# A hybrid decoder layer in one kernel: the beginning rebuilt, later GpSimd low parts, and GpSimd in the last scaling

## The chip, the cores and the metric

The kernel runs on one core of one Trainium2 chip. The metric is the time of one execution on the device in microseconds, median of several runs. Engines are named as in the profile: PE is TensorE's matmul (PEld its weight load), DVE VectorE, ACT ScalarE, POOL GpSimd, SP the engine that issues most transfers. Transfers are issued from SP's and from ACT's queue.

## What is computed

One layer of a hybrid decoder on x of 1024 tokens by 1024 channels, in float32:

```
h    = rmsnorm(x) * norm1_w
proj = h @ w_in                                  # q, k, v, z of mixer A; b, a; q, k, v of mixer B
A    = gated delta rule over 4 heads of 128: causal conv of width 4 and silu on q, k, v,
       l2norm of q and k, decay and beta per head, a triangular solve in each chunk,
       then rmsnorm times silu(z)
B    = attention over 8 heads of 64 in three dilated windows, merged by their denominators
x    = x + concat(A, B) @ w_out
u    = causal conv of width 3 over (rmsnorm(x) * norm2_w) @ w_up
x    = x + (silu(u_gate) * u_up) @ w_down
out  = rmsnorm(x) * final_norm_w
```

## The kernel before

All work lies with channels on the 128 partitions and tokens along the row; x comes transposed, as eight tiles of 128 x 1024. A float32 product is made from three products in a faster format: each operand is split into a high part (ACT copies it into that format) and a low part (the rest, a subtraction on DVE or POOL), and `mm3` (L200) adds high x high, high x low and low x high into a bank of PSUM. "Low part" below means the second.

**The order of the work.** Each engine runs its instructions in the order in which they were laid down. For PE that order is planned by the class `Weave` (L49): each part of the layer is a generator, which yields the time until its next product can run, and `Weave` picks by level and time. It keeps a model of the time: a product adds its `us` to PE's (`product`, L91); an operation on another engine adds an estimate to that engine's (`account`, L81; the estimates are in `Engine`, L124, and L151 to L158). So a changed estimate, or an operation given to another engine, can move products in PE's order anywhere behind it. On the other engines a scheduler orders by need; `after(inst, anchor)` (L189) forces one instruction behind another of the same engine, `ua` and `uv` (L154) are ACT and DVE with a raised priority.

**The beginning** (L242 to L365). SP issues norm1_w (`n1`), the first half of the first weights (`w0`, three column tiles of keys), the first x tile in two halves, the second half of the weights, and then x tiles and weights by turns. For each x tile, `split_x` (L286) makes `xhi` on ACT (scaled by n1) and `xlo` on DVE; ACT squares the tile and DVE adds it to `acc`, the sum of squares. Meanwhile PE multiplies a tile of ones 18 times (L351, the tile `warm`), which serves no result. `first` (L357) is the product of the first three key columns: for each of the eight x tiles six banks, three products each. `norms` (L371) turns `acc` into the reciprocal root of the mean square: a product with ones, a power on POOL, and a transposed broadcast that DVE copies into `rstdB` (L389). The columns leave their banks multiplied by `rstdB` (`scaled`, L445, the tiles `xr`), and only then are the banks free for the next columns.

**The dense columns** (`dense`, L498). 29 weights follow, in the order of `DENSE` (L45): one key, eight quarter weights for the values of mixer B, then q and v of the four heads by turns, the columns of attention, and z. `take` (L516) prepares the next weight while the present one is multiplied; from place 9 its low part is made by POOL (`spare`, L222), before that by DVE. Between the columns PE does what the planner puts there: transposes and small products of the delta rule (`kprep`, `qprep`, `vprep`, L602 and on), later attention. `forward_sub` inverts the triangles of all heads and chunks at once in 62 dependent DVE operations on two tiles in SBUF, `tmp` and `xi`, which interleave with the convolutions and the emptying of banks.

**The end** (`mlp_down`, L1535). The last product runs in halves of 256 tokens of the first 512. For each of eight channel tiles DVE adds the bank to x, ACT squares it, and the squares are added up (`complete`, L1486). `mean_of` (L1497) and `turned` (L1510) leave the reciprocal root, spread over the partitions, in a bank. `scale_out` (L1516) multiplies each of the eight pieces (128 x 256) by the final norm's weight `fw` and by that bank, one DVE operation each, and issues its transfer; for the last eight pieces the transfers go by turns to SP's and to ACT's queue.

Of the kernel before, what the change touches and what calls it, by code (L numbers as in the profile page):

```python
# [147 lines left out]
def hybrid_layer(tc, I, out):  # L148
# [93 lines left out]
    n1 = const("n1", [P, KT], I["n1"])  # L242
# [43 lines left out]
    def split_x(xt, k, sl):  # L286
        hi, lo = xs[k]
        ac.activation(hi[:, sl], xt[:, sl], AF.Copy, scale=n1[:, k:k + 1])
        ve.scalar_tensor_tensor(lo[:, sl], xt[:, sl], n1[:, k:k + 1], hi[:, sl].bitcast(F32), op0=OP.mult,
                                op1=OP.subtract)  # L290

    for k in range(KT):
        xt = A("xt", ("kT*", "dv*")[k % 2])
        xts.append(xt)
        if k % 2 == 0:
            wst = tile_(wp, [P, 2, 384], F32, "wst", "wst", 2)
            whi, wlo = [A(nm, "uy", F32R, (P, 2, 384)) if k < 4 else A(nm, "kt", F32R, (P, 2, 384))
                        for nm in ("whi", "wlo")]
            wk0.append((whi, wlo))
        xs.append((X("xhi"), X("xlo")))  # L300
        if k == 0:
            sy.dma_start(wst[:, 0, :], I["w0"][0, :, 0])
            for h in range(2):
                sy.dma_start(xt[:, half(h)], I["xT"][:P, half(h)])
            sy.dma_start(wst[:, 1, :], I["w0"][0, :, 1])
            split(wst[:, 0, :], whi[:, 0, :], wlo[:, 0, :])
            for h in range(2):
                split_x(xt, 0, half(h))
            split(wst[:, 1, :], whi[:, 1, :], wlo[:, 1, :])
        else:  # L310
            if k % 2 == 0:
                sy.dma_start(wst, I["w0"][k // 2])
            sy.dma_start(xt, I["xT"][k * P:(k + 1) * P, :])
            if k % 2 == 0:
                wlast = split(wst, whi, wlo)
            split_x(xt, k, slice(0, S))
        sq = A("sq", "qa")
        ac.activation(sq, xt, AF.Square)
        if k == 0:
            sq0 = sq  # L320
        elif k == 1:
            ve.tensor_tensor(acc, sq0, sq, op=OP.add)
        else:
            inst = ve.tensor_tensor(acc, acc, sq, op=OP.add)
            if k == 6:
                after(inst, first_lo, "the products wait for these weights")
        if k == 4:
            first_lo = wlast
# [22 lines left out]
    for _ in range(18):  # L351
        mm(wbank[:, :P], warm, warm, 0.3)
# [4 lines left out]
    def first():  # L357
        for k in range(KT):
            w = wk0[k // 2]
            for i in range(6) if k else (0, 2, 4, 1, 3, 5):  # L360
                yield wv.need(*xs[k], *w)
                m, h = divmod(i, 2)
                wm = [t[:, k % 2, m * P:(m + 1) * P] for t in w]
                mm3(pst[i], wm, [t[:, half(h)] for t in xs[k]], k == 0, k == KT - 1)
# [6 lines left out]
    def norms():  # L371
        yield wv.need(acc, slack=8.0)
# [125 lines left out]
    def dense():  # L498
# [17 lines left out]
        def take():  # L516
            w = nxt.pop()
            i = place[0] = place[0] + 1
            if i < len(srcs):
                nxt.append(weight(None, st=raw.pop(), spare=i >= 9))  # L520
# [965 lines left out]
    def complete(m, hh, sl, apart=False):  # L1486
# [4 lines left out]
        ac.activation(sq[:, sl] if m else rstdB[:, sp_], x, AF.Square)  # L1491
# [24 lines left out]
    def scale_out(hh, sl, pb, ms=range(8), queues=(sy,), anchor=None):  # L1516
        for m in ms:
            x = x1h[m][:, part(m, hh, sl)]
            inst = ve.scalar_tensor_tensor(x, x, fw[:, m:m + 1], pb[:, :sl.stop - sl.start], op0=OP.mult, op1=OP.mult)
# [15 lines left out]
    def mlp_down():  # L1535
# [36 lines left out]
        left, right = slice(0, 256), slice(256, 512)  # L1572
        for i in range(4):
# [10 lines left out]
        scale_out(0, right, turned(mean_of(0, right, "hf", more), right, "ch"), queues=(sy, sa))  # L1584
# [72 lines left out]
```

## Time and profile before

| | us |
|---|---|
| runs, median of 3 | 1204.37 (1203.77 to 1204.42) |
| the profiled execution's own time | 1206.67 |
| its span, from the first to the last instruction | 1204.6 |

The times in all lines are from that one profiled execution. A line of the timeline gives start, duration, engine, source line, operation, the tile written and those read, shapes, and in brackets how long the engine had been idle before and what ended it. Source lines are often those of a helper (L142 and L144 stand for every operation given to DVE, ACT, POOL and the queues; L193 for products, L197 for transposes), so tiles tell more than lines. In a table of windows a row gives the window, its length, then busy time and instructions of PE, PEld, DVE, ACT and POOL, the granted clock of PE (1.00 is full), the share of the DMA engines and GB/s.

### The profile page before, as it was taken

What the parts mean: (1) busy time and instruction counts of PE and PEld (TensorE: products, weight loads), DVE (VectorE), ACT (ScalarE), POOL (GpSimd) and SP (SyncE); (2) the same over time, 40 slices, a digit from 0 to 9 for tenths busy, and PEclk for the clock granted to TensorE, in tenths of its full rate; (3) what the DMA queues carried; (4) which work ended last, traced back from release to release, by engine and by line L of the source; (5) the groups of instructions that cost most, each with busy time, mean ns of one, the idle gap of its engine ahead of it and who ended that gap; (6) DMA issues with size and microseconds to landing.
All of it is one profiled execution on the core that took longest, in us unless ns stands there. A gap on an engine that the chain in (4) does not pass through costs nothing.

```text
span 1204.6 us, 18326 instructions
## 1 busy us (share of the span) xinstructions
PE 1191.6 (99%) x7068; PEld 987.0 (82%) x7068; DVE 916.1 (76%) x1442; ACT 575.3 (48%) x1126; POOL 108.2 (9%) x98
## 2 busy tenths in 40 slices
PE   9999999999999999999999999999999999999997
PEld 7888778889877778888888888888888888888886
DVE  7583985656365466767989989889898889999875
ACT  7375335456355443655545544444454454444441
POOL 0313232213422110000000000000000000000000
PEclk9999999999999999999999999999999999999998
DMA  7434233435624304444213122131322298547513
GB/s 235 107 93 121 103 109 119 149 115 164 222 94 128 95 36 120 169 140 140 84 56 106 58 100 91 67 105 53 105 73 85 94 370 305 180 162 226 165 54 140
DMA packets 85798, 154.80 MB, mean 129 GB/s; under 512 B 21168, under 2 KB 36304, under 8 KB 85712
## 3 DMA queue, kind: packets, MB, share of 16 engines
q1 hardware_dynamic: 85136, 153.12, 39.1%
q8 instruction: 55, 0.90, 0.3%
q10 hardware_dynamic: 576, 0.52, 0.1%
q14 instruction: 31, 0.25, 0.1%
HBM read 117.68 MB, written 35.93 MB: 128 GB/s over the span
## 4 chain that ended last, share of the span: by engine, by line
PE 93%; DVE 4%; ACT 1%; issue 1%; DMA 1%; SPq 0%; POOLq 0%; POOL 0%; DVEq 0%; ACTq 0%
PE ps L193 43%; PE pa L193 20%; PE dw L193 17%; PE pc L193 10%; PE ps L197 3%; DVE tmp L142 1%; DVE xi L142 1%; PE warm L193 1%; ACT sm L144 0%; DMA mt<-mdram 0%; DVE xr L142 0%; DVE qT L142 0%; DVE vT L142 0%; DMA mdram<-um 0%; DVE x1h L142 0%
## 5 line engine op out<-in xcount | busy, mean ns | idle before, releaser
L193 PE MATMUL dw<-pr 128*128 128x512 f32 (+1 forms) x984 | 211.3, 376 | 0.0
L193 PEld LDWEIGHTS dw<-pr 128*128 128x128 f32 x984 | 176.7, 188 | 33.6
L193 PE MATMUL ps<-xhi,whi 128*128 128x512 f32 x384 | 157.9, 411 | 0.5 <-DVE xr L142 0.5
L193 PE MATMUL ps<-xhi,wlo 128*128 128x512 f32 x384 | 150.5, 392 | 0.0
L193 PE MATMUL ps<-xlo,whi 128*128 128x512 f32 x384 | 150.3, 392 | 0.0
L193 PE MATMUL pa<-T,pair 128*128 128x512 f32 x528 | 127.0, 389 | 0.0
L193 PEld LDWEIGHTS pa<-T,pair 128*128 128x128 f32 x528 | 99.0, 188 | 20.6
L193 PEld LDWEIGHTS ps<-xhi,whi 128*128 128x128 f32 x384 | 72.7, 189 | 19.1 <-issue 5.6
L193 PEld LDWEIGHTS ps<-xhi,wlo 128*128 128x128 f32 x384 | 72.4, 188 | 15.8
L193 PEld LDWEIGHTS ps<-xlo,whi 128*128 128x128 f32 x384 | 72.7, 189 | 12.3
L142 ACT ACTIVATE u<-pa 128x512 f32<-128x512 f32 x44 | 26.3, 598 | 107.3 <-PE pa L193 107.3
L142 ACT ACTIVATE whi<-wst 128x1024 fp32r<-128x1024 f32 (+2 forms) x41 | 41.8, 1019 | 72.1 <-PE ps L193 40.3
L142 DVE SCALAR_TENSOR_TENSOR y<-xu,fcw,y 128x1023 f32<-128x1023 f32 (+1 forms) x44 | 56.4, 1281 | 22.1 <-ACT y L142 22.0
L142 POOL TENSOR_TENSOR rs<-rs,mhalf 128x2 f32<-128x2 f32 (+2 forms) x4 | 4.5, 1116 | 738.7 <-DVE rs L144 738.7
L193 PE MATMUL pc<-T,S 128*128 128x512 f32 x264 | 63.4, 389 | 0.0
L193 PE MATMUL pc<-B,pair 128*128 128x512 f32 x264 | 63.4, 389 | 0.0
L193 PE MATMUL pa<-B,A 128*128 128x512 f32 x264 | 63.4, 389 | 0.0
L193 PE MATMUL pa<-T,S 128*128 128x512 f32 x264 | 63.4, 389 | 0.0
L142 DVE TENSOR_TENSOR wst<-wst 128x512 f32<-128x512 f32 x88 | 60.5, 687 | 0.9
L193 PE MATMUL ps<-B,pair 128*128 128x512 f32 x252 | 60.5, 389 | 0.0
L144 ACT ACTIVATE sm<-sm,mx 128x128 f32<-128x128 f32 (+7 forms) x64 | 35.4, 555 | 47.9 <-DVE mx L144 47.9
L142 POOL TENSOR_TENSOR wlo<-wst,whi 128x1024 fp32r<-128x1024 f32 x20 | 47.9, 2393 | 115.6 <-ACT whi L142 113.7
(246 smaller groups left out, 2417.5 us busy)
## 6 DMA issues: line engine op xcount, KB each, us to landing
wst<-in_wu SPq DMA_DIRECT2D x44, 512.0 KB, 3.7
wd<-in_wd SPq DMA_DIRECT2D x44, 512.0 KB, 4.5
upark<-y SPq DMA_DIRECT2D x22, 512.0 KB, 3.7
wst<-in_wi SPq DMA_DIRECT2D x21, 512.0 KB, 3.7
r<-upark SPq DMA_DIRECT2D x11, 512.0 KB, 7.8
r<-upark SPq DMA_DIRECT2D x22, 256.0 KB, 6.8
wa<-in_wd SPq DMA_DIRECT2D x22, 256.0 KB, 3.1
wst<-in_wv SPq DMA_DIRECT2D x8, 512.0 KB, 3.7
```

What stands on the lines that cost most here:

```text
L142: return getattr(eng, op)(*a, **kw)
L144: return getattr(eng, op)(*a, **kw)
L193: tc.stamp_issue_order_token(nc.tensor.matmul(dst, lhs, rhs, start=start, stop=stop, **kw).ins, TOKEN)
L197: tc.stamp_issue_order_token(nc.tensor.transpose(dst, src, ident if idt is None else idt).ins, TOKEN)
```

## The change

Four things are edited.

- The beginning. `n1` and both halves of the first weights are issued from ACT's queue; SP begins with the first x tile. The splits get a raised priority and a fixed order on ACT. The square of tile k comes behind the splits of tile k + 2, and so does its sum on DVE; the last two follow at the end. The warming products fall from 18 to 9, and their time in the planner's model from 0.3 to 0.43 each. For the first two x tiles the products with `xlo` come behind the others of their group of banks. The norm's place in the plan is 9.5 instead of 8.0 behind the sum of squares.
- In `take`, POOL makes low parts from place 17 on instead of 9. Places 9 to 16, the q and v columns, get theirs from DVE.
- In the last `scale_out`, pieces 3 and 6 are multiplied by `fw` on ACT ahead (behind the last square), ACT copies the bank into SBUF (`pbs`), and POOL multiplies both pieces by it. DVE scales the other six.
- `complete` remembers its last square, so that ACT's two early multiplications can be put behind it.

```diff
--- before.py
+++ after.py
@@ -239,7 +239,8 @@
     def wk(src, st=None):
         return [t.rearrange("p (k m) -> p k m", k=KT) for t in weight(src, st=st)]
 
-    n1 = const("n1", [P, KT], I["n1"])
+    n1 = const("n1", [P, KT])
+    sa.dma_start(n1, I["n1"])
     mhalf = const("mhalf", [P, NCH])
     ve.memset(mhalf, -0.5)
     phalf = const("phalf", [P, NCH])
@@ -285,9 +286,30 @@
 
     def split_x(xt, k, sl):
         hi, lo = xs[k]
-        ac.activation(hi[:, sl], xt[:, sl], AF.Copy, scale=n1[:, k:k + 1])
-        ve.scalar_tensor_tensor(lo[:, sl], xt[:, sl], n1[:, k:k + 1], hi[:, sl].bitcast(F32), op0=OP.mult,
-                                op1=OP.subtract)
+        inst = ua.activation(hi[:, sl], xt[:, sl], AF.Copy, scale=n1[:, k:k + 1])
+        if k == 0:
+            after(inst, his[0] if sl.start else whis[0], "in the order of arrival")
+        if k == 1:
+            after(inst, whis[1], "the weights come first")
+        his[k:] = [inst]
+        lo_of[0] = uv.scalar_tensor_tensor(lo[:, sl], xt[:, sl], n1[:, k:k + 1], hi[:, sl].bitcast(F32), op0=OP.mult,
+                                           op1=OP.subtract)
+
+    def split_first(src, hi, lo):
+        whis.append(ua.activation(hi, src, AF.Copy))
+        return uv.tensor_tensor(lo, src, hi.bitcast(F32), op=OP.subtract)
+
+    his, los, lo_of, sqs, whis = [], [], [None], [], []
+
+    def square(k, hi, lo):
+        sq = A("sq", "qa")
+        late = "the products wait for the splits first"
+        after(ac.activation(sq, xts[k], AF.Square), hi, late)
+        sqs.append(sq)
+        if k == 1:
+            after(ve.tensor_tensor(acc, sqs[0], sq, op=OP.add), lo, late)
+        elif k > 1:
+            after(ve.tensor_tensor(acc, acc, sq, op=OP.add), lo, late)
 
     for k in range(KT):
         xt = A("xt", ("kT*", "dv*")[k % 2])
@@ -299,33 +321,26 @@
             wk0.append((whi, wlo))
         xs.append((X("xhi"), X("xlo")))
         if k == 0:
-            sy.dma_start(wst[:, 0, :], I["w0"][0, :, 0])
+            for j in range(2):
+                sa.dma_start(wst[:, j, :], I["w0"][0, :, j])
             for h in range(2):
                 sy.dma_start(xt[:, half(h)], I["xT"][:P, half(h)])
-            sy.dma_start(wst[:, 1, :], I["w0"][0, :, 1])
-            split(wst[:, 0, :], whi[:, 0, :], wlo[:, 0, :])
+            split_first(wst[:, 0, :], whi[:, 0, :], wlo[:, 0, :])
             for h in range(2):
                 split_x(xt, 0, half(h))
-            split(wst[:, 1, :], whi[:, 1, :], wlo[:, 1, :])
+            split_first(wst[:, 1, :], whi[:, 1, :], wlo[:, 1, :])
         else:
             if k % 2 == 0:
                 sy.dma_start(wst, I["w0"][k // 2])
             sy.dma_start(xt, I["xT"][k * P:(k + 1) * P, :])
             if k % 2 == 0:
-                wlast = split(wst, whi, wlo)
+                split_first(wst, whi, wlo)
             split_x(xt, k, slice(0, S))
-        sq = A("sq", "qa")
-        ac.activation(sq, xt, AF.Square)
-        if k == 0:
-            sq0 = sq
-        elif k == 1:
-            ve.tensor_tensor(acc, sq0, sq, op=OP.add)
-        else:
-            inst = ve.tensor_tensor(acc, acc, sq, op=OP.add)
-            if k == 6:
-                after(inst, first_lo, "the products wait for these weights")
-        if k == 4:
-            first_lo = wlast
+        los.append(lo_of[0])
+        if k > 1:
+            square(k - 2, his[k], los[k])
+    for k in (KT - 2, KT - 1):
+        square(k, his[-1], los[-1])
 
 
     ident = const("ident", [P, P], I["ident"])
@@ -348,8 +363,8 @@
 
 
     wbank = bank("atr", "warm")
-    for _ in range(18):
-        mm(wbank[:, :P], warm, warm, 0.3)
+    for _ in range(9):
+        mm(wbank[:, :P], warm, warm, 0.43)
 
 
     pst = [bank(t) for t in ("hf", "asc", "ch") for _ in range(2)]
@@ -357,11 +372,24 @@
     def first():
         for k in range(KT):
             w = wk0[k // 2]
-            for i in range(6) if k else (0, 2, 4, 1, 3, 5):
+            if k < 2:
+                for group in ((0, 2, 4), (1, 3, 5)) if k == 0 else (range(6),):
+                    for low in range(2):
+                        for i in group:
+                            m, h = divmod(i, 2)
+                            wm = [t[:, k % 2, m * P:(m + 1) * P] for t in w]
+                            hi, lo = [t[:, half(h)] for t in xs[k]]
+                            if low:
+                                mm(pst[i], wm[0], lo, 0.2135, False, False)
+                            else:
+                                mm(pst[i], wm[0], hi, 0.2135, k == 0, False)
+                                mm(pst[i], wm[1], hi, 0.2135, False, False)
+                continue
+            for i in range(6):
                 yield wv.need(*xs[k], *w)
                 m, h = divmod(i, 2)
                 wm = [t[:, k % 2, m * P:(m + 1) * P] for t in w]
-                mm3(pst[i], wm, [t[:, half(h)] for t in xs[k]], k == 0, k == KT - 1)
+                mm3(pst[i], wm, [t[:, half(h)] for t in xs[k]], False, k == KT - 1)
         wv.done.add("first")
 
 
@@ -369,7 +397,7 @@
     rstdB = const("rstdB", [P, S])
 
     def norms():
-        yield wv.need(acc, slack=8.0)
+        yield wv.need(acc, slack=9.5)
         ssp = yield from next_bank("atr", acc)
         for c in range(NCH):
             mm(ssp[:, c:c + 1], acc[:, c * P:(c + 1) * P], ones[:, :1], 0.215)
@@ -517,7 +545,7 @@
             w = nxt.pop()
             i = place[0] = place[0] + 1
             if i < len(srcs):
-                nxt.append(weight(None, st=raw.pop(), spare=i >= 9))
+                nxt.append(weight(None, st=raw.pop(), spare=i >= 17))
             if i + 1 < len(srcs):
                 raw.append(raw_weight(srcs[i + 1]))
             return w
@@ -1488,7 +1516,7 @@
         sp_ = part(m, hh, sl)
         x = x1h[m][:, sp_]
         sq = tile_(sp, [P, 512], F32, "sq3", "t2", 2)
-        ac.activation(sq[:, sl] if m else rstdB[:, sp_], x, AF.Square)
+        last["sq"] = ac.activation(sq[:, sl] if m else rstdB[:, sp_], x, AF.Square)
         if apart:
             return sq
         if m:
@@ -1513,10 +1541,18 @@
             tp(pb[:, c * P:(c + 1) * P], rs[:, c:c + 1].to_broadcast([P, P]))
         return pb
 
-    def scale_out(hh, sl, pb, ms=range(8), queues=(sy,), anchor=None):
+    def scale_out(hh, sl, pb, ms=range(8), queues=(sy,), anchor=None, shared=()):
+        n_ = sl.stop - sl.start
+        if shared:
+            pbs = tile_(sp, [P, n_], F32, "pbs", "t2", 2)
+            ac.activation(pbs, pb[:, :n_], AF.Copy)
         for m in ms:
             x = x1h[m][:, part(m, hh, sl)]
-            inst = ve.scalar_tensor_tensor(x, x, fw[:, m:m + 1], pb[:, :sl.stop - sl.start], op0=OP.mult, op1=OP.mult)
+            if m in shared:
+                po_.tensor_tensor(x, x, pbs, op=OP.mult)
+                queues[m % len(queues)].dma_start(out[m * P:(m + 1) * P, part(m, hh, sl)], x)
+                continue
+            inst = ve.scalar_tensor_tensor(x, x, fw[:, m:m + 1], pb[:, :n_], op0=OP.mult, op1=OP.mult)
             if anchor is not None:
                 after(inst, anchor, "the sums of the last banks go first")
             queues[m % len(queues)].dma_start(out[m * P:(m + 1) * P, part(m, hh, sl)], x)
@@ -1570,6 +1606,7 @@
             return total, complete(4 + i, 0, sl, sl.start > 0 and i == 3)
 
         left, right = slice(0, 256), slice(256, 512)
+        shared = (3, 6)
         for i in range(4):
             last_product(i, left)
         last_product(0, right)
@@ -1581,7 +1618,10 @@
         scale_out(0, left, pl, range(4, 6), anchor=third)
         fourth, more = last_product(3, right)
         scale_out(0, left, pl, range(6, 8), anchor=fourth)
-        scale_out(0, right, turned(mean_of(0, right, "hf", more), right, "ch"), queues=(sy, sa))
+        for m in shared:
+            x = x1h[m][:, part(m, 0, right)]
+            after(ac.activation(x, x, AF.Copy, scale=fw[:, m:m + 1]), last["sq"], "the last squares go first")
+        scale_out(0, right, turned(mean_of(0, right, "hf", more), right, "ch"), queues=(sy, sa), shared=shared)
 
     wv.add(0, norms())
     wv.add(1, gates())
```

## The prediction

> **What bounds the kernel now.** First the head of the page and its line of busy time, then the chain of work that ended last.
>
> ```profile
> span 1204.6 us, 18326 instructions
> ...
> PE 1191.6 (99%) x7068; PEld 987.0 (82%) x7068; DVE 916.1 (76%) x1442; ACT 575.3 (48%) x1126; POOL 108.2 (9%) x98
> ...
> PE 93%; DVE 4%; ACT 1%; issue 1%; DMA 1%; SPq 0%; POOLq 0%; POOL 0%; DVEq 0%; ACTq 0%
> ```
>
> TensorE (PE) is the bound nearly everywhere. An edit pays only where PE works on nothing useful or waits. The table of windows finds these places; its columns are the window, its length, and the busy time of PE, PEld, DVE, ACT and POOL.
>
> ```profile
> 0.00:7.83 7.83, 6.73 (x36) 6.73 (x37) 1.84 (x7) 3.55 (x5) 0.51 (x5) 1.00 0.67 193
> 7.83:1195.27 1187.44, 1183.11 (x7025) 979.03 (x7024) 909.74 (x1425) 571.35 (x1121) 107.05 (x92) 1.00 0.39 128
> 1195.27:1204.60 9.33, 1.73 (x10) 1.20 (x10) 4.47 (x12) 0.42 (x1) 0.69 (x1) 0.65 0.51 168
> ```
>
> Up to 7.83 us PE runs only warming products. Then it is idle for 1187.44 - 1183.11 = 4.3 us in all. The last 9.33 us are norm, scaling and transfers. So the change's three parts can win at most 7.8, some 4.3 plus slow clock, and some part of 9.3 us. The waits of PE say where the 4.3 lie:
>
> ```profile
> PE ps L197 <- DVE at L142: 1.6, 1, 1.6
> ...
> PE ps L193 <- DVE xr L142: 0.5, 1, 0.5
> ...
> PE ps L193 <- DVE ct L144: 0.5, 1, 0.5
> PE ps L197 <- DVE gq L142: 0.3, 1, 0.3
> ```
>
> DVE's at, xr and gq (1.6 + 0.5 + 0.3 = 2.4 us) all fall between 137 and 153.5 us, where the q, v columns and the forward substitution share DVE. The windows there, and the two in which PE warms up:
>
> ```profile
> 1.10:6.60 5.50, 5.50 (x26) 5.50 (x26) 1.31 (x2) 2.15 (x3) 0.00 (x0) 1.00 0.74 200
> 6.60:7.83 1.23, 1.23 (x12) 1.23 (x12) 0.26 (x1) 1.02 (x2) 0.00 (x0) 1.00 0.97 331
> ...
> 127.50:150.00 22.50, 21.87 (x108) 17.72 (x107) 21.98 (x35) 8.73 (x23) 7.26 (x3) 1.00 0.22 71
> 150.00:153.54 3.54, 1.69 (x10) 0.98 (x8) 3.47 (x14) 0.05 (x2) 0.71 (x1) 1.00 0.00 0
> 153.54:156.95 3.41, 3.41 (x11) 2.83 (x11) 2.34 (x7) 2.37 (x9) 0.00 (x0) 0.50 0.38 154
> ```
>
> DVE is full from 127.5 to 153.5 (21.98 of 22.50, then 3.47 of 3.54): there it, not PE, sets the pace. After the wait the granted clock (sixth figure behind the length) is 0.50 for 3.41 us, which costs 1.7 us more. The middle thus holds 2.4 + 1.7 = 4.1 us.
>
> **The beginning.** Removed: nine of 18 warming products; n1 and two weight transfers go from SP's queue to ACT's, so the first x half is SP's first transfer; squares go two tiles behind their splits; in tiles 0 and 1 the products with xlo go last.
>
> ```profile
> 1.10 6.97 PE L193 MATMUL warm<-warm 128*128 128x128 f32 x36 [1.10 <-DVE ones L142]
> ```
> ```profile
> 1.64 0.90 SPq L142 DMA_DIRECT2D xt<-in_xT  x2
> ```
> ```profile
> 3.76 0.52 ACT L142 ACTIVATE whi<-wst 128x384 fp32r<-128x384 f32 x1 [1.76 <-DMA wst<-in_w]
> 4.57 0.72 ACT L142 ACTIVATE xhi<-xt,n 128x512 fp32r<-128x512 f32 x1 [0.28 <-DMA xt<-in_xT]
> 6.81 0.72 ACT L142 ACTIVATE xhi<-xt,n 128x512 fp32r<-128x512 f32 x1 [1.52 <-DMA xt<-in_xT]
> ```
>
> A warming product is two passes (x36 for 18). Before 6.60 a pass takes 5.50/26 = 0.21 us, so 18 passes end at 1.10 + 18 x 0.21 = 4.9. The inputs: the weight's high part is made at 3.76 now, and I leave it there, since on ACT's queue it stands behind n1 as it does now on SP's; x's half lands earlier (issued at about 0.7 instead of 1.64), so xhi follows whi at once, at 4.28, and ends at 5.0. With hops I take 5.3 for the first product. The xlo half, now last in its group, is no longer needed first. The next rows give the pace: 13 products start between 22.68 and 25.40, 2.72/12 = 0.227 us apart; at the clock of 0.50 they start 0.42 apart.
>
> ```profile
> 22.68 0.39 PE L193 MATMUL ps<-xhi,wlo 128*128 128x512 f32 x1
> ...
> 25.40 0.39 PE L193 MATMUL ps<-xhi,wlo 128*128 128x512 f32 x1
> ```
> ```profile
> 155.67 0.63 PE L193 MATMUL ps<-xhi,whi 128*128 128x512 f32 x1
> 156.09 0.63 PE L193 MATMUL ps<-xlo,whi 128*128 128x512 f32 x1
> ```
>
> The passes become twice as fast at 6.60 (26 in 5.50 us, then about ten in 1.23), so until there products run at the slow pace: (6.60 - 5.30)/0.42 = 3.1, then 1.23/0.227 = 5.4, together 8.5 products of 0.227 done by 7.83: **-1.9 us**. The bounds: PE starts at 4.9 at full pace, -2.9; or the inputs come only when the second x half comes now (6.81 + 0.72 = 7.53), -0.3. Second x half: needed after nine products, about 7.9, there now at 7.53 and then earlier; no wait. If ACT's table load stood ahead of its three DMA issues they would start 1.28 us later; I put that into the lower bound.
>
> Does the head start survive? The first banks are emptied with rstdB, which needs the sums of squares that now come last on DVE.
>
> ```profile
> 26.96 1.22 DVE L142 TENSOR_TENSOR acc<-acc,sq 128x1024 f32<-128x1024 f32 x1
> ...
> 41.97 0.69 DVE L142 COPY rstdB<-ps 128x512 f32<-128x512 f32 x1
> ...
> 46.78 3.41 DVE L142 TENSOR_TENSOR xr<-ps,rstdB 128x512 f32<-128x512 f32 x5 [0.92 <-PE ps L193]
> ```
>
> rstdB is whole at 42.66, its first reader waits for PE until 46.78: 4.1 us of cover. The head start takes 1.9, the norm's later place in the plan (slack 9.5 for 8.0) 1.5. The cover shrinks to about 0.7; the order of squares adds at most one sum of 1.22 to the end of acc, which the norm, waiting for its place in the plan, hides. I count nothing; a miss costs its amount beyond 0.7.
>
> **The late low parts.** Eight dense weights (places 9 to 16) get their low part from DVE instead of POOL. The prices of one, then what stands in the full stretch:
>
> ```profile
> L142 DVE TENSOR_TENSOR wlo<-wst,whi 128x1024 fp32r<-128x1024 f32 x16 | 19.6, 1224 | 8.6 <-ACT whi L142 8.6
> ```
> ```profile
> 127.64 2.53 POOL L142 TENSOR_TENSOR wlo<-wst,whi 128x1024 fp32r<-128x1024 f32 x1 [7.73 <-ACT whi L142]
> 140.88 2.50 POOL L142 TENSOR_TENSOR wlo<-wst,whi 128x1024 fp32r<-128x1024 f32 x1 [10.71 <-ACT whi L142]
> ```
> ```profile
> 127.95 2.46 DVE L142 TENSOR_TENSOR tmp<-mt,xi 128x220 f32<-128x220 f32 x1
> 130.45 0.39 DVE L142 TENSOR_TENSOR xi<-xi,tmp 128x220 f32<-128x220 f32 x1
> ...
> 141.02 0.68 DVE L142 TENSOR_TENSOR xr<-ps,rstdB 128x512 f32<-128x512 f32 x1
> 141.62 2.04 DVE L142 TENSOR_TENSOR xi<-xi,tmp 128x255 f32<-128x255 f32 x1
> ```
>
> A 220-wide operation takes 0.39 alone, but 2.46 when it starts under POOL's low part, and it ends just after POOL. The 255-wide one takes 2.04; it would take about 0.42. Both have two SBUF inputs. The xr at 141.02, with one input in PSUM, keeps its 0.68. So POOL's two low parts ahead of the big wait hold DVE for 2.07 + 1.62 = 3.7 us, and DVE's own would take 2 x 1.22 = 2.4: DVE is **1.2 us** further at 151.7. PE's 2.4 us of waits fall by that. With 2.9 instead of 1.69 of 3.54 us busy, I expect the clock not to fall: another 1.7. Against this stands that PE's order is planned anew (the plan's time for warming falls from 5.4 to 3.9 us, eight low parts move between its engines); I allow two new waits, 0.7 in all, near the 0.5 of the wait for ct above. Middle: -1.2 - 1.7 + 0.7 = **-2.2**. Bounds: all of it gone, -4.1; or none of DVE's holds is given back and three low parts weigh fully on PE with a second slow window, 3 x 1.22 + 1.7 = +5.4. The other six low parts stand where PE hardly waits: nothing.
>
> **The end.** DVE scales six of the last pieces, not eight; ACT multiplies pieces 3 and 6 by fw ahead, and copies the bank; POOL multiplies. ACT's two early copies lie in its idle time after the last square. DVE's share falls by two eighths:
>
> ```profile
> 1198.42 3.22 DVE L142 SCALAR_TENSOR_TENSOR x1h<-x1h,fw,ps 128x256 f32<-128x256 f32 x8 [1.42 <-PE ps L197]
> ```
> ```profile
> L142 POOL TENSOR_TENSOR wlo<-wst,whi 128x1024 fp32r<-128x1024 f32 x20 | 47.9, 2393 | 115.6 <-ACT whi L142 113.7 <-PE ps L197 1.8
> ```
> ```profile
> 1199.84:1203.10 3.26, 0.00 (x0) 0.00 (x0) 1.81 (x5) 0.00 (x0) 0.00 (x0) 0.50 0.96 316
> ```
>
> That is 0.8 us of DVE. But what is late next is the transfer: from 1199.84 to 1203.10 the 16 DMA engines are 96% busy, with eight pieces of 128 KB; 0.96 x 3.26 = 3.1 us of work. The first piece comes no sooner. So the end can come at most 0.1 sooner: **-0.1**. POOL's piece, a quarter of 2393 ns, is 0.6 us, so two end near 1200.3 after ACT's copy; even at 1.2 each (no size effect below half) they end at 1201.5, hardly later than DVE's last piece now (1201.64). Each POOL piece has others behind it on its queue: 5 and 7 wait behind 3 on ACT's. I hold the cost within +0.5.
>
> **Sum.** -1.9 - 2.2 - 0.1 = -4.2. The profiled execution took 1206.67 us (2.07 outside its span); 1202.5. The median of the runs is 2.30 below it: **1200.2**.
>
> **The rivals.**
> - *DVE is not relieved.* The operations that meet POOL's low parts change with every order; if the next ones read PSUM, as xr does, nothing was held and the middle gives nothing: -1.9 - 0.1 = -2.0, 1202.4. For it: only two holds decide. Against: nearly every operation of the substitution has two SBUF inputs. With it I put the case that ACT's queue delivers late and the start gains nothing while the middle does (-2.3, 1202.1). Together 0.19.
> - *The clock opens one window later.* A wait of 0.4 between warming and products, in the window that should open it. The window row at 150.00 shows that 1.69 of 3.54 us was not enough. One 3.41 us window more puts the opening at 10.0: 4.7/0.42 = 11.2 products by then, against 2.17/0.227 = 9.6 now, so the start gives 0.4, the whole -2.7, 1201.7: 0.08. This is what the Trainium skill's page "TensorE: Matmul & The Clock Gate" (What's actually happening) warns of: the clock is set by free-running windows of some 3.4 us, each judged by its own activity. Of the trace, the 3.41 us row at 0.50 agrees with it.
> - *DVE becomes the bound, slower.* In the full stretch three low parts of 1.22 us stand in DVE's queue ahead of the operations that free PE's banks, and the holds by POOL were only idle time moved. PE's waits grow by 3.7 and a second slow window adds 1.7: +5.4 - 2.0 = +3.4, 1207.8. It decides from the point at which DVE's net gain of 1.2 turns into a loss of over 2.0. For it: 21.98 of 22.50 us busy. Against: the two holds. 0.13.
>
> **How the numbers follow.** The forecast has 0.60. A measurement here tells 0.2%, 2.4 us, from no change, so 1201.96 and 1206.78 are the limits. Faster: forecast and clock, 0.68; same: 0.19; slower: 0.13. The range takes the bounds of start and middle downward (-2.9 - 4.1 - 0.1 = -7.1, about 1197) and the cases without gain in the middle upward, with half a us for POOL's pieces and a miss at rstdB: 1205.
>
> **What would show it.** Start: the first product at 5.1 to 5.8 with a pace of 0.42 until the clock opens; wrong if ACT waits for a DMA beyond 5. Carry: no PE wait for xr near 45. Middle: no DVE operation of over 2 us beside a low part before 160, no window at 0.50; wrong if PE's waits for DVE exceed 2.4. End: last scaling near 1200.9, but the last bytes still about 4.6 us after the first scaling starts; wrong if the end moves with DVE.

## The result and the profile after

The changed kernel takes 1202.28 us (median of 16 runs, 1201.33 to 1203.32), the kernel before beside it 1205.03 us (16 runs, 1203.67 to 1208.60). The ratio is 0.9977, with a 95% interval of 0.9971 to 0.9984: faster by 2.75 us or 0.23%, where 1200.2 was forecast. The profiled execution took 1201.91 us.

The head of the page, the busy times and the chain of waits of the changed kernel answer to the first lines shown of before:

```profile
span 1200.0 us, 18298 instructions
...
PE 1186.8 (99%) x7050; PEld 982.8 (82%) x7050; DVE 914.4 (76%) x1448; ACT 575.9 (48%) x1129; POOL 90.4 (8%) x92
...
PE 93%; DVE 2%; DMA 2%; ACT 1%; issue 1%; POOL 0%; ACTq 0%; DVEq 0%; POOLq 0%; SPq 0%
```

PE is the bound as before. The table of windows, cut at the first product and at the first of the last scalings, and then the middle row of the same cut of the kernel before:

```profile
0.00:6.12 6.12, 3.84 (x18) 3.65 (x19) 0.84 (x6) 2.47 (x4) 0.51 (x5) 1.00 0.71 216
6.12:1193.84 1187.72, 1183.01 (x7032) 979.17 (x7032) 911.16 (x1437) 573.47 (x1126) 88.46 (x85) 1.00 0.40 128
1193.84:1199.97 6.13, 0.00 (x0) 0.00 (x0) 2.44 (x6) 0.00 (x0) 1.41 (x2) 0.50 0.51 171
```

```profile
7.83:1198.42 1190.59, 1184.84 (x7035) 980.24 (x7033) 910.99 (x1428) 571.76 (x1122) 107.74 (x93) 1.00 0.39 128
```

The start is 1.7 us shorter, the stretch behind it 2.9, and what follows the first scaling equal (6.13 and 6.18). Of the 2.9, idle time is 5.8 - 4.7 = 1.0; the other 1.8 is PE's busy time, which the window at half clock had lengthened. PE's waits in the changed kernel, one by one:

```profile
PE ps L193 <- ACT xhi L144: 1.2, 1, 1.2
...
PE ps L197 <- POOL rs L142: 1.1, 1, 1.1
PE ps L193 <- DVE wlo L144: 0.6, 1, 0.6
PE ps L193 <- ACT w L144: 0.5, 1, 0.5
PE ps L193 <- DVE ct L144: 0.4, 1, 0.4
PE ps L193 <- ACT sq L144: 0.4, 1, 0.4
```

The waits for at, xr and gq (2.4 us) are gone. Three are new: for xhi between the warming and the first product, for wlo near 23 us, and for sq (ACT, line 144) near 67 us.

Where the time came from is best seen by laying the two PE streams side by side: each product is counted at its usual distance to the next, and one reads when each trace reaches the same sum of work. Points and differences, worked out from the starts of PE's products:

| work done by PE, us | before | after | difference |
|---|---|---|---|
| 0.1 (first product) | 7.97 | 6.27 | -1.70 |
| 25 (behind the wait for wlo) | 36.94 | 36.10 | -0.84 |
| 50 | 62.10 | 61.42 | -0.68 |
| 60 (behind the wait for sq) | 72.38 | 72.20 | -0.18 |
| 118 | 130.73 | 130.55 | -0.18 |
| 135 | 149.04 | 147.61 | -1.43 |
| 142 | 159.94 | 154.67 | -5.27 |
| all (last product) | 1198.00 | 1192.97 | -5.03 |
| end of the span | 1204.6 | 1200.0 | -4.6 |

So nearly all of the head start of 1.7 us is given back by 72 us, the middle brings 5.1, and the end gives 0.4 back. This is one execution of each kernel: 4.6 us between their spans, where the medians differ by 2.75. The runs below show which part belongs to the one execution of before.

**The beginning.** The timeline of the changed kernel:

```profile
4.93 0.52 ACT L144 ACTIVATE whi<-wst 128x384 fp32r<-128x384 f32 x1 [1.52 <-DMA wst<-in_w]
5.36 1.32 ACT L144 ACTIVATE xhi<-xt,n 128x512 fp32r<-128x512 f32 x2
...
6.12 0.50 PE L193 MATMUL ps<-xhi,whi 128*128 128x512 f32 x1 [1.18 <-ACT xhi L144]
...
6.46 0.40 PE L193 MATMUL ps<-xhi,wlo 128*128 128x512 f32 x1
6.69 0.40 PE L193 MATMUL ps<-xhi,whi 128*128 128x512 f32 x1
```

ACT waits for the weights until 4.93 (3.76 before), so PE begins at 6.12 and not at 5.3. From the second product on, starts are 0.23 apart: the clock is already at full rate, where 0.42 had been forecast until 6.60.

**The middle.** The windows answer to the rows at 127.50, 150.00 and 153.54 of before; the rows of DVE to those at 127.95 and 141.62:

```profile
127.50:150.00 22.50, 22.50 (x116) 19.03 (x115) 22.18 (x45) 8.59 (x22) 1.75 (x1) 1.00 0.24 73
150.00:160.00 10.00, 10.00 (x48) 8.33 (x47) 9.42 (x17) 4.65 (x11) 0.00 (x0) 1.00 0.26 99
```
```profile
129.05 1.22 DVE L142 TENSOR_TENSOR wlo<-wst,whi 128x1024 fp32r<-128x1024 f32 x1
130.19 0.39 DVE L142 TENSOR_TENSOR xi<-xi,tmp 128x231 f32<-128x231 f32 x1
...
138.86 1.22 DVE L142 TENSOR_TENSOR wlo<-wst,whi 128x1024 fp32r<-128x1024 f32 x1
139.99 0.42 DVE L142 TENSOR_TENSOR xi<-xi,tmp 128x256 f32<-128x256 f32 x1
...
148.15 0.86 DVE L142 SCALAR_TENSOR_TENSOR at<-ps,bp,dec 128x128 f32<-128x128 f32 x3
```

PE is never idle and no window stands at 0.50. DVE is as full as before (22.18 of 22.50), but does 45 operations in that time instead of 35: no operation takes over 1.6 us between 120 and 210 us, where before six did. The last of the eight at ends at 149.0; before they ended as late as this:

```profile
152.31 1.12 DVE L142 SCALAR_TENSOR_TENSOR at<-ps,bp,dec 128x128 f32<-128x128 f32 x4
```

**The end.** The last products and scalings of the changed kernel:

```profile
1192.70 0.69 PE L197 MATMUL ps<-ident,rs 128*128 128x128 f32 x2 [1.10 <-POOL rs L142]
1193.43 0.38 ACT L142 ACTIVATE pbs<-ps 128x256 f32<-128x256 f32 x1 [1.68 <-PE ps L197]
1193.84 2.44 DVE L142 SCALAR_TENSOR_TENSOR x1h<-x1h,fw,ps 128x256 f32<-128x256 f32 x6 [1.97 <-ACT pbs L142]
1193.89 1.41 POOL L142 TENSOR_TENSOR x1h<-x1h,pbs 128x256 f32<-128x256 f32 x2 [1.24 <-ACT pbs L142]
```

DVE is at work for 2.44 us instead of 3.22, but the bracket says what it waited for: not for the bank (PE), but for ACT's copy of the same bank.

### The profile page after: what moved, and what is told of

The parts are those of the page before. It is cut to its first block, busy times and chain, and to the rows that moved or that the text cites. A ratio compares the mean times of both kernels' runs of the same rounds, so it can differ in the third digit from the quotient of the medians.

```text
span 1200.0 us, 18298 instructions
## 1 busy us (share of the span) xinstructions
PE 1186.8 (99%) x7050; PEld 982.8 (82%) x7050; DVE 914.4 (76%) x1448; ACT 575.9 (48%) x1129; POOL 90.4 (8%) x92
## 4 chain that ended last, share of the span: by engine, by line
PE 93%; DVE 2%; DMA 2%; ACT 1%; issue 1%; POOL 0%; ACTq 0%; DVEq 0%; POOLq 0%; SPq 0%
PE ps L193 44%; PE pa L193 20%; PE dw L193 17%; PE pc L193 10%; PE ps L197 3%; DMA wst<-in_w 1%; DVE kT L142 1%; ACT sm L144 0%; DVE xr L142 0%; DMA wba<-in_wba 0%; PE pd L193 0%; DVE zz L142 0%; ACT dec L142 0%; DVE x1h L142 0%; ACT xr L142 0%
## 5 line engine op out<-in xcount | busy, mean ns | idle before, releaser
L142 ACT ACTIVATE whi<-wst 128x1024 fp32r<-128x1024 f32 x36 | 38.3, 1063 | 67.7 <-PE ps L193 54.8
L193 PEld LDWEIGHTS pa<-T,S 128*128 128x128 f32 x264 | 49.5, 188 | 10.3
```

The source lines that it names most:

```text
L142: return getattr(eng, op)(*a, **kw)
L193: tc.stamp_issue_order_token(nc.tensor.matmul(dst, lhs, rhs, start=start, stop=stop, **kw).ins, TOKEN)
```

## The experiments

| kernel | median, us (range, runs) | before beside it | ratio [95%] |
|---|---|---|---|
| changed kernel | 1202.28 (1201.33-1203.32, 16) | 1205.03 | 0.9977 [0.9971, 0.9984] |
| e1, beginning alone | 1204.93 (1203.82-1207.62, 11) | 1205.61 | 0.9994 [0.9985, 1.0003] |
| e2, low parts alone | 1201.84 (1201.10-1202.97, 6) | 1205.61 | 0.9967 [0.9955, 0.9979] |
| e3, end alone | 1205.33 (1204.74-1207.82, 11) | 1205.61 | 1.0000 [0.9991, 1.0009] |
| e4, all but the end | 1201.79 (1201.22-1204.10, 6) | 1205.61 | 0.9968 [0.9957, 0.9980] |
| e5, new plan, POOL as before | 1205.69 (1204.11-1206.53, 11) | 1205.38 | 1.0001 [0.9993, 1.0010] |
| e6, old plan, DVE makes them | 1202.25 (1200.95-1203.03, 9) | 1205.38 | 0.9976 [0.9966, 0.9985] |
| e7, a bank of its own | 1202.19 (1200.55-1204.06, 10) | 1205.38 | 0.9976 [0.9966, 0.9985] |
| e8, weights sooner | 1201.46 (1200.73-1203.31, 9) | 1205.38 | 0.9974 [0.9965, 0.9984] |
| e9, plan kept, no shared end | 1201.71 (1200.91-1203.07, 11) | 1204.91 | 0.9977 [0.9968, 0.9986] |
| e10, the same with e7's end | 1201.97 (1201.51-1202.29, 11) | 1204.91 | 0.9976 [0.9968, 0.9985] |
| e11, all low parts on DVE | 1203.81 (1202.63-1204.49, 11) | 1204.91 | 0.9991 [0.9982, 1.0000] |
| e12, e6 with at as late as before | 1204.19 (1202.16-1204.81, 11) | 1205.22 | 0.9988 [0.9979, 0.9997] |

Theory at the outset: the gain is that POOL no longer holds DVE in the substitution. Rivals: it is PE's order, planned anew; or it is the beginning.

### The parts alone: e1 to e4

e1 is the changed kernel with `spare=i >= 9` and the last scaling of before; e2 the kernel before with this one line; e3 the kernel before with the shared scaling; e4 the changed kernel without it.

```diff
-                nxt.append(weight(None, st=raw.pop(), spare=i >= 9))
+                nxt.append(weight(None, st=raw.pop(), spare=i >= 17))
```

> The beginning alone (low parts from place 9 on POOL, the last scaling all on DVE). Reading of the two traces: PE starts 1.7 us sooner, but waits 0.8 us for a low part of the weights near 23 us and 0.5 us near 66 us, so 0.2 us are left by 115 us, and the waits between 137 and 153 us stay as before; within 0.7 us of before. The prediction: 1.9 us faster, of which nothing is lost on the way.

> Low parts of places 9 to 16 on DVE alone, beginning and end as before. Reading of the traces: this carries nearly all of the change, 2.5 to 5 us faster, with no DVE operation over 2 us and no PE wait over 1 us between 120 and 200 us; how much of it the slow clock of 1.7 us adds depends on how often before has it. The prediction: 2.2 us faster. Rival (DVE is the bound): no gain or slower, with longer PE waits near 150 us.

> The shared last scaling alone. Reading of the traces: the first DVE scaling starts 0.4 us later, because it waits for ACT's copy of the bank, and the eight transfers still take 3.1 us; 0.2 to 0.5 us slower. The prediction: 0.1 us faster. If DVE's time set the end: 0.8 us faster.

> Beginning and low parts, the last scaling all on DVE. Reading of the traces: 0.2 to 0.5 us faster than with all parts, so 3 to 3.5 us faster than before. The prediction: 0.1 us slower than with all parts.

Measured: the low parts alone make the whole gain (0.9967), and neither the beginning nor the end is told apart from no change by its interval. In the trace of e1 the lead over before is 1.23 us at the first product and -0.06 at 118 us of work. e4 showed the rival of the late clock. In its profiled execution (1204.10, the longest of its six) PE idles longer ahead of the first product, and then does half as many instructions in the same time. The row of e4's window, and the same window of the changed kernel:

```profile
6.80:13.10 6.30, 6.15 (x15) 4.80 (x16) 5.23 (x7) 5.49 (x8) 0.00 (x0) 1.00 1.02 410
```
```profile
6.80:13.10 6.30, 6.30 (x30) 5.17 (x29) 4.62 (x6) 5.17 (x6) 0.00 (x0) 1.00 1.02 411
```
```profile
6.95 0.79 PE L193 MATMUL ps<-xhi,whi 128*128 128x512 f32 x1 [1.63 <-ACT xhi L144]
7.54 0.63 PE L193 MATMUL ps<-xhi,wlo 128*128 128x512 f32 x1
7.97 0.63 PE L193 MATMUL ps<-xhi,whi 128*128 128x512 f32 x1
```

15 instructions instead of 30, 0.43 apart until 13.1 us: e4's first product comes 0.8 later than the changed kernel's, and at equal work e4 then stays 2.8 behind. The granted clock in these rows is 1.00 all the same, since the trace's record of it begins with its first change (in e4 at 13.10), so it is the distance of the starts, the last three rows, that shows the rate.

### Which half of the low parts: e5, e6, e12

The line changes two things: who subtracts, and what the planner books. e5 lets POOL do it and books DVE; it was meant to have the work of before and the plan of e2. e6 is the reverse:

```diff
+    vp = Engine(wv, nc.vector, "gpsimd", 0.15, 0.0021)
...
-            po_.tensor_tensor(lo, st, hi.bitcast(F32), op=OP.subtract)
+            (spare if spare is not True else po_).tensor_tensor(lo, st, hi.bitcast(F32), op=OP.subtract)
...
-                nxt.append(weight(None, st=raw.pop(), spare=i >= 9))
+                nxt.append(weight(None, st=raw.pop(), spare=i >= 9 and (vp if i < 17 else True)))
```

> Before, with places 9 to 16 still made by POOL, but entered in the planner's model as DVE's: PE's order is that of e2_low_parts, the work that of before. Theory (POOL's low parts hold DVE): the DVE operations of over 2 us stay and so does a PE wait for DVE near 150 us; within 1 us of before. Rival (the new order of PE's products is what gains): 3 to 4 us faster, as e2_low_parts.

> Before, with places 9 to 16 made by DVE, but entered in the planner's model as POOL's: PE's order is that of before, the work that of e2_low_parts. Theory (holds): 3 to 5 us faster, no DVE operation over 2 us between 120 and 200 us, no PE wait for ACT near 66 us, since that came with the new order. Rival (the order gains): within 1 us of before.

e6 gains all (0.9976), e5 nothing (1.0001). e5's timeline shows the same holds as before, its list of PE's waits the same wait; in e6's list from 115 to 160 us nothing is left.

```profile
127.38 2.64 POOL L142 TENSOR_TENSOR wlo<-wst,whi 128x1024 fp32r<-128x1024 f32 x1 [7.73 <-ACT whi L142]
127.80 2.48 DVE L142 TENSOR_TENSOR tmp<-mt,xi 128x231 f32<-128x231 f32 x1
```
```profile
PE ps L198 <- DVE at L142: 1.6, 1, 1.6
PE ps L198 <- DVE gq L142: 0.3, 1, 0.3
```

The order planned anew is out, and more plainly than these two runs were built to show: the booking moves nothing. As far as tile names and shapes tell (buffer numbers are left out), PE's products stand in one order in the kernel before, e2, e3, e5, e6, e11 and e12 (6294 products; those of 32 rows or columns, which start nearly together, are left aside). The changed kernel's order differs from it only ahead of 44 us. On DVE, ACT and POOL, too, e5 has the order of the kernel before, and e6 that of e2. So e5 and e6 are repeats of those two kernels: they show again that the gain goes with the engine that subtracts, and no new order of PE was ever there to gain.

But the hold is too small by itself: it gives DVE 3.7 - 2.4 = 1.2 to 1.3 us, and the eighth at starts 27.6 us behind the first step of the substitution in e6 and 31.5 in the kernel before, 3.9 sooner. DVE's order has changed too: ahead of the first and of the fifth at stand 35 and 37 operations of the substitution (`tmp`, `xi`) in the changed kernel, e2 and e6, but 40 and 43 in the kernel before, e1, e3 and e5. The order on DVE goes with the engine that makes the low parts. Five of 0.4 are 2 us of the rest. e12 is e6 with the old order of these operations forced:

```diff
+                if steps and h == 0 and c == 0:
+                    after(inst, steps[39 if c0 == 0 else 42], "as in the order before")
...
+            steps.extend([st_a, st_b])
```

> DVE makes the eight late low parts and the planner's order is that of the kernel before, as in e6; but DVE's eight products at of the first head are forced behind as many steps of the forward substitution as in the kernel before: 40 ahead of the first, 43 ahead of the fifth (35 and 37 in e6, in which the eighth at starts 27.6 us behind the first step; 31.5 in the kernel before). Theory A (the gain has two halves: 1.3 us that POOL no longer holds DVE, and 2.2 us because five steps now stand behind at): the eighth at starts 29.7 to 30.1 behind the first step, PE waits for at and gq again, 0.6 to 1.5 in all, and the median is 1203.0 to 1204.0. Theory B (the hold alone; the order on DVE is of no matter): no wait of PE from 137 to 155 us, median 1202.3 as in e6.

Theory A holds but for the size. The eighth at starts 29.74 us behind the first step; PE waits for at again, though not for gq:

```profile
152.82 0.66 PE L198 MATMUL ps<-ident,vT 128*128 128x128 f32 x4 [1.48 <-DVE at L142]
```

The median is 1204.19, 0.2 above what A allowed, and with 0.9988 [0.9979, 0.9997] against e6's 0.9976 about half of the gain is lost; the two intervals overlap a little. By the traces, from 118 to 150 us of work, e12 gains 3.0 and e6 4.9 on the profiled execution of before; e3 (the middle of before, but without the window at half clock) gains 2.4 on it. So without that window the hold alone is worth about 0.6 us and the place of at about 1.9. The 0.6 is less than the 1.3 that DVE saves, because the substitution itself begins later: its first step stands at 122.68 us in e12 and 120.72 in e3, 2.0 later, while PE is 0.8 later at 118 us of work. The new place of at with POOL's holds kept was not run, so this split holds for the one order in which the two were taken away.

### The end: e7

ACT copies from a second bank into which the broadcast is made again:

```diff
-        scale_out(0, right, turned(mean_of(0, right, "hf", more), right, "ch"), queues=(sy, sa), shared=shared)
+        rs = mean_of(0, right, "hf", more)
+        pr_ = turned(rs, right, "ch")
+        scale_out(0, right, pr_, queues=(sy, sa), shared=shared, own=turned(rs, right, "hf"))
```

> After, with the last broadcast made twice, into a second bank from which ACT copies for POOL. If DVE's first scaling waits because ACT reads the same bank, it starts 0.4 us sooner and the end is 0.3 to 0.4 us sooner than after; if it waits for something else, the end stays as after. The eight transfers take 3.1 us either way, so the end is no sooner than with all scaling on DVE by more than 0.2 us.

```profile
1192.45 1.66 DVE L142 SCALAR_TENSOR_TENSOR x1h<-x1h,fw,ps 128x256 f32<-128x256 f32 x4 [1.30 <-PE ps L197]
1192.67 0.38 ACT L142 ACTIVATE pbs<-ps 128x256 f32<-128x256 f32 x1 [1.65 <-PE ps L197]
```

DVE now waits for PE. Measured from the start of the last product of the squares with ones:

| | first scaling | DVE's last ends | last bytes land | span ends |
|---|---|---|---|---|
| before | +1.94 | +5.16 | +7.04 | +8.11 |
| changed kernel | +2.49 | +4.93 | +7.54 | +8.61 |
| e3 (end alone) | +2.45 | +4.89 | +7.51 | +8.58 |
| e4 (DVE alone) | +1.82 | +5.04 | +6.93 | +8.00 |
| e7 (own bank) | +1.82 | +4.26 | +6.90 | +7.97 |

Against e4, e7 frees DVE 0.78 us sooner and ends 0.03 sooner: the transfers set the end. The changed kernel and e3 start 0.5 to 0.7 later for the copy than the kernel before and e4, and end as much later. Over all 14 profiles the span ends at +7.99 to +8.26 with DVE alone (nine), at +8.37 to +8.61 with the shared bank (three) and at +7.97 with a bank of its own (two), so the copy costs 0.1 to 0.6. The medians (1202.19 and 1202.28) can't tell 0.6 us.

### The beginning: e8

The first weights go ahead of `n1` on ACT's queue, and the weights of tiles 4 to 7 get a place of their own, so that their transfer can start sooner.

```diff
-    sa.dma_start(n1, I["n1"])
...
-            wst = tile_(wp, [P, 2, 384], F32, "wst", "wst", 2)
+            wst = tile_(wp, [P, 2, 384], F32, "wst", "wst", 2) if k < 4 else A("wst", "ev", F32, (P, 2, 384))
...
+                if j == 0:
+                    sa.dma_start(n1, I["n1"])
```

> After, with the first weights issued ahead of n1 on ACT's queue, and the last two weights of the first product in slots of their own, so that their transfers wait for no low part. Theory (the head start is lost later, in waits for the weights' low part near 23 us and for ACT near 66 us): first product at 5.0 to 5.5 instead of 6.1, no wait near 23, but one of up to 1 us near 66; 0.5 to 1.3 us faster than after. The prediction's step (a head start carries to the end): 1.5 to 2 us faster than after.

```profile
4.43 0.52 ACT L144 ACTIVATE whi<-wst 128x384 fp32r<-128x384 f32 x1 [1.02 <-DMA wst<-in_w]
...
5.25 1.34 ACT L144 ACTIVATE xhi<-xt,n 128x512 fp32r<-128x512 f32 x2 [0.29 <-DMA n<-in_n]
...
6.03 0.50 PE L193 MATMUL ps<-xhi,whi 128*128 128x512 f32 x1 [0.72 <-ACT xhi L144]
...
11.05 0.50 PE L193 MATMUL ps<-xhi,whi 128*128 128x512 f32 x1 [0.63 <-ACT xhi L144]
```

whi comes 0.5 sooner, but xhi now waits for n1, so the first product starts at 6.03 and not at 5.0 to 5.5. The second half of the weights comes later too (its whi starts at 9.43, in the changed kernel at 7.93); the next xhi stands behind it on ACT and makes PE wait at 11, and at 118 us the lead is 0.08. The wait near 23 us is gone and nothing is won. The median, 1201.46, isn't told apart from 1202.28 by the intervals.

### Putting it together: e9, e10, e11

e9 is the changed kernel with e6's booking and no shared end; e10 the same with e7's end; e11 is e6 with the low parts from place 17 on made by DVE too.

> The changed kernel, but the planner books the eight late low parts as POOL's (the order of the kernel before for the columns), DVE makes them, and DVE alone scales at the end. Theory (the gain is that POOL no longer holds DVE; the order planned anew only brings the wait for ACT's square near 66 us): the wait of 0.4 to 0.6 us near 66 is gone, no DVE operation over 1.6 us from 60 to 210, the last transfer about 0.5 sooner behind the last square than in the changed kernel; the median 1201.2, 1.1 below the changed kernel (1202.28), and the head start that is left at 118 us is about 0.6 instead of 0.2. Rival (any lead of the beginning is given back, wherever PE waits next): another wait takes its place ahead of 118 us, and the median is that of the kernel whose low parts alone were moved, 1201.8 to 1202.3.

> As the one before, with the end shared again but ACT copying from a bank of its own. If the transfers set the end, it ends behind the last square within 0.1 us of DVE alone (last landing +6.9, end +8.0), and the median agrees with the one before within 0.5 us. If DVE's scalings set it, six instead of eight take 0.8 us off it.

> The kernel before, with the low parts of all places from 9 on made by DVE, booked as POOL's. Theory (a hold of DVE costs only where DVE sets PE's pace, from 127 to 153 us): the twelve low parts from place 17 on, from 210 us, bring nothing more; median 1202.2 as with the eight alone, within 0.5 us. Rival (DVE held by POOL costs PE later too): below 1201.5. Other rival (12 x 1.22 us more on DVE delay attention): above 1203.

As the booking moves nothing, e9 has on every engine the order of e4, and e10 that of e7: they repeat those kernels, and the theory put on record for e9, that the plan brings the wait for sq near 67 us, is wrong. In e9 the wait is there (0.4), and of the lead, expected at 0.6, there is 0.06 left at 118 us. The wait differs between executions of one order: none in the kernel before and 0.75 in e5, none in e6 and 0.75 in e2. What goes with it in all 14 profiles is the time that DVE takes from the first xr (45.6 to 48.8 us) to gel, which ACT needs for its squares: 14.2 us in the kernel before, e3, e6 and e11, without the wait; 14.75 in the changed kernel, e7 to e10, with 0.43; 14.8 to 14.9 in e4 and e1 with 0.5 and 0.6; 15.05 in e2, e5 and e12 with 0.75. The difference is how many operations on `kT` lie under POOL's selects of `dec`. Rows of DVE in e6, then in e12:

```profile
52.07 6.76 DVE L142 SCALAR_TENSOR_TENSOR kT<-xr,gcw,kT 128x1023 f32<-128x1023 f32 x4
...
61.16 0.16 DVE L142 COPY gel<-dec 128x8 f32<-128x8 f32 x1
```
```profile
51.81 7.59 DVE L142 SCALAR_TENSOR_TENSOR kT<-xr,gcw,kT 128x1023 f32<-128x1023 f32 x4
...
61.74 0.16 DVE L142 COPY gel<-dec 128x8 f32<-128x8 f32 x1
```

One such operation takes 1.28 us alone and 2.1 under a select; e6 has two of the long ones in this row, e12 three. So here too POOL holds DVE. That is read from the rows; moving the selects was not tried, and why they fall differently from one execution to the next stays open.

e9 and e10 (1201.71 and 1201.97) agree with the changed kernel and with e2 within their intervals: no kernel here is shown to beat it. In e10 the last bytes land at +6.90 and in e9 at +6.92 behind the last product of the squares, as the theory of the transfers has it. e11 bears out its second rival: twelve more low parts on DVE lose 1.6 us against e6 by the medians; its lead over before, by the traces, falls from 5.4 us at 200 us of work to 3.6 at 400. Why there in detail stays open.

## Why the prediction was right or wrong

The sign, the place and the hold of DVE by POOL were right; the time was 2.1 us too low. Of that, 1.4 is the change (-4.2 forecast, -2.75 measured) and 0.7 the base: three runs gave 1204.37 for the kernel before, 16 gave 1205.03. By the profile pair the forecast sum of -4.2 came close (1206.67 to 1201.91, -4.8), but by luck, through errors that cancel.

- **Beginning, -1.9 forecast, -0.2 kept.** The step "the weight's high part is made at 3.76 now, and I leave it there" failed: 4.93. On ACT's queue the weights come later than on SP's, and putting them ahead of n1 (e8) gets back 0.5 of the 1.2. That PE was 1.7 ahead at the first product all the same came from the clock: it was fully open at 4.41 us here, and in the kernel before only at 6.77, so that there the warming products held PE until 7.83. In the six other profiles with the old beginning the first product starts at 6.53 to 7.03; on these the lead is 0.4 to 0.9. The larger failure is "Does the head start survive? ... I count nothing". I tested it against one reader, rstdB, and that cover held (whole at 45.4, first read at 46.08). But the next operands (wlo at 23, 0.9 of the lead; sq at 67, 0.5) had their own times, set by transfers and by DVE, and took the lead away. The old beginning loses its leads in the same way: e3, e6 and e12 start 1.1 to 1.3 us ahead of the kernel before and then wait 0.8 for xlo near 12 us.
- **Middle, -2.2 forecast, -5.1 in the profile pair.** That DVE is 1.2 us further was right. "PE's 2.4 us of waits fall by that" failed in two ways. It took DVE's order as given; five steps of the substitution moved behind at, worth more than the hold (e12). And 2.4 was read too small: a wait row counts from the end of the last product's record, 0.39 long, while products start 0.227 apart, so each stall behind one costs PE some 0.16 more than its row says. From start to start the stalls for xr, gq and at in before sum to 2.4 + 3 x 0.16 = 2.8 us. The allowance of +0.7 for new waits had no ground in the plan: behind 44 us PE's order didn't change, and the middle has no new wait. And of the 5.1, 2.3 to 2.6 belong to the one profiled execution of before: so much do e1, e3 and e5, whose middle is that of before, gain on it from 118 to 150 us of work. They lack its slow clock and its wait for xr. Against these three the changed middle gains 2.5 to 2.8, about the 2.75 of the medians, where the forecast without its 1.7 for the clock has 0.5.
- **POOL's hold.** It was read rightly from two long rows, and e5 and e6 bear it out. The Trainium skill's page "SBUF — State Buffer" (SBUF: two separate sides) calls the port pair that GpSimd shares with VectorE an exclusive lock: whichever of a GpSimd operation that reads SBUF and a VectorE operation with two SBUF inputs starts first has it for its whole length. The rows agree: 0.39 becomes 2.46, and xr, with an input in PSUM, keeps 0.68.
- **Slow clock, -1.7.** The window at 0.50 is gone. But none of e1, e3, e5 and e12, which all keep the wait for at of 1.5 to 1.6 us, has it in its profile: it belongs to some executions only (the last section says which). I took its 1.7 off the profiled time and then "the median of the runs is 2.30 below it" off again, so it was counted twice. Without it: 1206.67 - 2.5 - 2.30 = 1201.9, against 1202.28; that this is near is again luck, as the middle and the beginning in that -2.5 are both mis-sized.
- **End, -0.1 forecast, +0.4 in the profile pair.** The bound by the transfers was right (e4 against e7: 0.03). What failed is that ACT's copy was priced only for POOL's pieces; DVE's first scaling was put behind the copy of the same bank. The +0.5 that was held in reserve covers what it cost (0.1 to 0.6 over the profiles).
- **Rivals.** "DVE is not relieved" fell with e2 and e6. "The clock opens one window later" happened, not here but in two of the seven profiles with nine warming products: in e4 two windows later (13.1 us, PE stood 1.63 us ahead of its first product, 1.9 lost beside the later first product) and in e10 one (10.1 us, 1.6 of the lead lost). 0.08 was too little for it; in none of the seven with 18 did PE's first product meet the slow clock. This agrees with what the Trainium skill's page "TensorE: Matmul & The Clock Gate" (What's actually happening) says of windows judged by their own activity. "DVE becomes the bound" didn't come with eight low parts; with twenty (e11) part of the gain is lost, and whether by DVE stays open.

## What to carry to other kernels

Where two engines' rows lengthen each other, moving the work is worth not only the overlap but also the order that the moved work leaves on the engine; look up what then stands ahead of the operation that the bound engine waits for, and price that. A head start is kept only as far as every later operand comes sooner too: follow it through the next few stalls, not only the first. Before a stall is taken off a profiled time, ask whether the median run has it at all. And when an edit is meant to change an order, compare the order in the two traces first: here the planner's booking moved no product.

## What the runs showed of the hardware that was not expected

- The time at which PE reaches full rate differs between executions: 4.0 to 6.8 us in the seven profiles with 18 warming products (6.8 in that of before, the latest), ahead of the first product (6.0 to 6.6) in five with nine, 10.1 and 13.1 in e10 and e4. A part of what the profile pair shows of the start is therefore chance.
- Within a trace the granted clock changes only at whole steps of 3.413 us from its first change: in the kernel before at 6.77, 153.54 (43 steps), 156.95 (44) and 1198.02 us (349), and so in all 14. Counted by each trace's own steps, what matters is where a wait falls. In the kernel before the waits for gq (0.3) and at (1.6) lay within one step and left PE 1.57 us of work in it; the next step ran at half clock. In e3 a step ends between the same two waits, at 151.07 us, and the clock stayed. The row of the kernel before, then two of e3:

```profile
150.12:153.54 3.42, 1.57 (x9) 0.86 (x8) 3.35 (x13) 0.01 (x1) 0.59 (x1) 1.00 0.00 0
```
```profile
147.66:151.07 3.41, 3.12 (x17) 2.20 (x16) 3.38 (x11) 1.06 (x1) 2.17 (x1) 1.00 0.00 0
151.07:154.49 3.42, 1.88 (x11) 1.63 (x11) 3.21 (x12) 1.84 (x8) 0.00 (x0) 1.00 0.33 133
```

- Steps with 1.9 to 2.2 us of work in e1, e3, e5 and e12 were not followed by the slow clock, that with 1.57 was. At the start of the traces, full rate came behind a step with at least 2.88 us of work (e9) and not behind one with 2.74 or less (e4: 2.45, then 2.74; e10: 2.63). These are 14 profiles; a limit between such figures is not shown.
- `n1`, 4 KB in 128 small packets, held ACT's queue for about a microsecond: in the changed kernel, beside the first x tile on SP's queue, its packets ran from 2.17 to 3.23 us and those of the weights behind it from 3.21 to 4.48. In the kernel before, where `n1` is first on SP's queue, they ran from 1.73 to 2.13 and from 2.22 to 3.40.
